# Squared activations without the norm's factor, a smaller setup table in PSUM, one norm step per gated step, and 28 six-product pairs with ten Strassen pairs, in a two-layer S5 and attention encoder

## The chip, the cores and the metric

One core of one Trainium2 chip runs the whole program. The metric is the time of one execution in device microseconds (us), the median of several runs. Shorter names of the engines: PE (TensorE, matrix products), DVE (VectorE), ACT (ScalarE), POOL (GpSimd), SP (SyncE, which here only issues DMA transfers).

## The reference

Two layers on a residual stream of 256 tokens by 2048 channels, all in float32. Layer 0 mixes tokens with a bidirectional diagonal state space (S5), followed by a gated linear unit (GLU); layer 1 with windowed attention. A dense MLP follows each. Every part has an RMS norm ahead of it and a residual addition behind it:

```python
def rms_norm(x, gain):
    y = x * lax.rsqrt(jnp.mean(x * x, axis=-1, keepdims=True) + NORM_EPS)
    return y * gain

def s5_mixer(u, a_re, a_im, log_step, b_re, b_im, c_re, c_im, d_skip, w_glu_a, w_glu_b):
    step = jnp.exp(log_step)[..., None]
    mag = jnp.exp(ar * step)
    lb_re = mag * jnp.cos(ai * step)
    lb_im = mag * jnp.sin(ai * step)
    den = ar * ar + ai * ai
    ...
    z = jax.nn.gelu(y)
    return (z @ w_glu_a) * jax.nn.sigmoid(z @ w_glu_b)

def sqrelu_mlp(h, w_up, w_down):
    return jnp.square(jax.nn.relu(h @ w_up)) @ w_down

for i in range(2):
    h = h + (s5_mixer, windowed_gqa)[i](rms_norm(h, ...), ...)
    h = h + sqrelu_mlp(rms_norm(h, mlp_norm[i]), mlp_w_up[i], mlp_w_down[i])
```
`w_up` is 2048 x 8192 and `w_down` 8192 x 2048, so one MLP reads 128 MB of weights.

## The kernel before

**Products.** A float32 product is made of three matmuls: each factor is split into a high part (a cast) and a low part (the rest), and high x high, low x high and high x low are summed in PSUM (`mm`, L983 to L987). Every weight tile of 128 x 2048 (1 MB) is loaded by SP in a fixed order (`fetch`, L670), cast by ACT (L692) and its low part taken by DVE (L693) or, for 6 and 7 "forms", in `wload_fast` (L696 to L714). The load runs one tile ahead of its use (`wnext`).

**The order** in which each engine runs its instructions is laid out by a planner when the program is built, from the order of the calls and from its own estimates of time. `issue_after` adds an order between two instructions; `interleave` mixes generators of work by rates.

**S5** (0 to some 230 us). `s5_setup` makes tables of powers of the state's factors: `tables()` works out exponential, sine and cosine on DVE and ACT, interleaved with the input norm `norm()`, whose sum over tokens is a matmul (L326) followed by L328; the sine and cosine steps end in L275. `powers()` makes the powers and then three products of them for each half of the partitions (`tab`: L406, L407 and a copy), and copies the first 64 columns into PSUM (`tabp`). `out_tables` prepares further tables on POOL, with a reciprocal on DVE (L435). Then `s5_a(0)` (first half of the groups; products on DVE, L506, eight blocks), a sequential scan on DVE (`s5_scan`), beside it `s5_a(1)` with the products on POOL, the second scan, and the output part.

**GLU** (to 380 us). `glu_rest` runs four blocks of 512 columns. While block cb's products run, the post-processing of block cb-1 is mixed in at rate 0.7 (L874): `glu_post` has four steps, two that gate, add to the residual and start the next norm (`norm_pre`), and two that transpose the result for the MLP and split it into parts (`norm_post`, L758, L761). Block 3 has nine steps, `glu_tail` last.

**MLP** (`mlp`, called twice). The inputs are multiplied by the norm's gain alone; the factor per token, `rstd`, is put in later. `rstd_row` (L772) lays it along the free axis: two diagonal matrices times a matrix of ones on PE (L779). The up phase has 64 blocks of 128 rows of the hidden layer (`up_mm`: L895 and L897, 16 matmuls each). `up_post` turns one block into its activation: ACT copies one part (L902), DVE adds it to the other, DVE takes the maximum with 0 and multiplies by the row of factors (L903), ACT squares (L905).

The down-projection works on 32 *pairs* of such blocks. In a pair the operands form a 2 x 2 matrix of blocks, so four products in eight block multiplications (24 matmuls with the three per block). Strassen's form has seven (21 matmuls): `FORMS`. Six of these (18 matmuls, `SIXTH`) complete a pair of the first half of the columns except for one block of products, which is done later for four pairs at once. Two passes cover the two halves of the columns:

- *Up phase*: `SIX` puts the six products of pairs 0 to 23 behind up blocks 6, 8, 10, 13, 15, 17, 20 and so on, two or three blocks apart.
- *Pass one* (half 0): `PASS[0]` lists 14 items. A negative number is a tile of `wp2`, which holds the left-out products of four six-product pairs (12 matmuls for one tile); the rest are pairs 24 to 31 in plain form (24).
- *Pass two* (half 1): all 32 pairs, nine of them (`FAST`) in Strassen's form.

Strassen's sums stand in four PSUM banks of their own and are added to the residual once in each pass: in pass one by `fold0` (DVE), in pass two by `fold`, which works out four sums on DVE and lets POOL issue accumulating DMAs into the residual (L1027 to L1034). `end` adds the plain sums (L1040), and behind the second MLP stores the output. `norm_end` works out `rstd` for the next part.

Of the kernel before, what the change touches and what calls it, by code (L numbers as in the profile page):

```python
# [10 lines left out]
F32 = mybir.dt.float32  # L11
# [3 lines left out]
ALU = mybir.AluOpType  # L15
AX = mybir.AxisListType

P = 128
# [164 lines left out]
class Kernel:  # L183
# [109 lines left out]
    def s5_setup(self):  # L293
# [14 lines left out]
        self.tab = ar.get("tab", [3, T, G], at=44032)  # L308
# [61 lines left out]
        def tables():  # L370
            are, aim, lst = prm[:, 0], prm[:, 1], prm[:, 2]
            tb4, tb3 = (self.bank().rearrange("p (k g) -> p k g", k=4) for _ in range(2))
            mag, xr, xi, sn, cs = (tp.tile([P, G], F32, name=n) for n in ("mag", "xr", "xi", "sn", "cs"))
# [12 lines left out]
            v.tensor_mul(lam[:, 1, 1], mag, sn)  # L386

        def powers():
            lam, t2 = self.lam, self.t2

            for o, x, n in ((2, 1, 1), (3, 1, 2)):
                ov, av = lam[:, :, o:o + n], lam[:, :, x:x + n]
                br, bi = (lam[:, i:i + 1, x + n - 1:x + n].broadcast_to([P, 2, n, G]) for i in range(2))
                tv = t2[:, :, 0:n]
                v.tensor_mul(ov, av, br)
                v.tensor_mul(tv, av, bi)
                v.tensor_sub(ov[:, 0], ov[:, 0], tv[:, 1])
                v.tensor_add(ov[:, 1], ov[:, 1], tv[:, 0])
            H = P // 2
            tab = self.tab  # L400
            for lo in (0, H):
                s = slice(lo, lo + H)
                lr = lam[s, 0, 1:T + 1][:, ::-1] if lo else lam[s, 0, 1:T + 1]
                li = lam[s, 1, 1:T + 1][:, ::-1] if lo else lam[s, 1, 1:T + 1]
                a.copy(tab[s, 1], lr)
                v.scalar_tensor_tensor(tab[s, 0], lr, -1.0, li, op0=ALU.mult, op1=ALU.subtract)  # L406
                v.tensor_sub(tab[s, 2], li, lr)  # L407
# [11 lines left out]
        u_trans(0)  # L419
        with self.tc.issue_after(self.rs.ins):  # L420
            powers()
        ar.free("xc", "sq", "gn", "dd")

        def out_tables():
# [10 lines left out]
            v.reciprocal(den, den)  # L435
# [24 lines left out]

    def s5_a(self, h):
# [7 lines left out]
        def statein(b, pin):  # L469
            for i in range(0, 8, 4):  # L470
# [11 lines left out]
                if h == 0 and i:  # L482
                    v.tensor_copy(o, bv)
                else:
                    self.evac = a.copy(o, bv)
# [12 lines left out]
        for b in range(8):  # L498
# [3 lines left out]
            for k, src in ((0, bc[:, 1]), (1, bs), (2, bc[:, 0])):  # L502
                tb = self.tabp[k][:, :, g0:g0 + 8] if h == 0 else tab[:, k, :, g0:g0 + 8]
                tb = tb.rearrange("p t (g o) -> p g t o", o=1).broadcast_to([P, 8, T, 16])
                sb = src.rearrange("p g (o c) -> p g o c", o=1).broadcast_to([P, 8, T, 16])
                e.tensor_mul(q[:, :, k], tb, sb)  # L506
                if k == 2:
                    fetch(b + 3)
                yield
# [262 lines left out]
    def rstd_row(self, rb):  # L772

        nc = self.nc
        bk = self.bank()
        for tt in range(2):
            dg = self.small.tile([P, P], F32, name="dg")
            nc.vector.tensor_scalar_mul(dg, self.ident, self.rstd[:, tt:tt + 1])
            nc.tensor.matmul(bk[:, tt * P:(tt + 1) * P], lhsT=self.ones, rhs=dg, start=True, stop=True)  # L779
        nc.vector.tensor_copy(rb, bk[:, :L])  # L780
# [77 lines left out]
    def glu_rest(self):  # L858
        post = None
        for cb in range(4):  # L860
# [17 lines left out]
    def mlp(self, nxt, fin):  # L878
# [4 lines left out]
        rb = pool.tile([P, L], F32, name="rb", bufs=1)  # L883
# [15 lines left out]
        def up_post(fb, bk):  # L899
# [3 lines left out]
            nc.vector.scalar_tensor_tensor(s, s, 0.0, rb, op0=ALU.max, op1=ALU.mult)  # L903
# [65 lines left out]
        def split(kp, a, fast):  # L969
            n = a.shape[1] // 2  # L970
            if kp < 0:
                k = -1 - kp
                h = hTs[0][:, 8 * k + 1:8 * k + 8:2, :P] if k < 4 else hTs[1][:, 8 * k - 31:8 * k - 24:2, :P]
                return halves(a, h, n)
# [34 lines left out]

        def fold0():  # L1010
            p1, q5, q6, q7 = (bks[n] for n in ("p1", "q5", "q6", "q7"))
            v.tensor_add(rs(0, 0), rs(0, 0), p1)
            nc.scalar.copy(ssix, p1)
            v.tensor_sub(ssix, ssix, q6)
            v.tensor_add(rs(0, 1), rs(0, 1), ssix)
            v.tensor_sub(rs(0, 1), rs(0, 1), q5)
            v.tensor_sub(ssix, q7, ssix)
            v.tensor_add(rs(1, 0), rs(1, 0), ssix)
            v.tensor_add(ssix, ssix, q5)
            v.tensor_add(rs(1, 1), rs(1, 1), ssix)  # L1020

        def fold():
            f = ar.get("fo", [4, 512], at=37888)
            c, d, u, w = (f[:, i] for i in range(4))
            g = nc.gpsimd
# [4 lines left out]
            g.dma_start(rs(0, 1), w, accum_op=ALU.add)  # L1030
            v.tensor_sub(u, bks["q7"], u)
            g.dma_start(rs(1, 0), u, accum_op=ALU.add)
            v.tensor_add(d, u, bks["q5"])
            g.dma_start(rs(1, 1), d, accum_op=ALU.add)  # L1034
            ar.free("fo")

        def end(half, t, j):
            cb = half * 2 + j
            cs = slice(cb * 512, (cb + 1) * 512)
            v.tensor_add(self.resid[:, t, cs], self.resid[:, t, cs], bks["x%d" % (2 * t + j + 1)])  # L1040
# [43 lines left out]
        aform = Ring([ar.get("af#%d" % i, [1024], F32R, at=27648 + 1024 * i) for i in range(4)])  # L1084
        more = [extra(at, F32R) for at in (23552, 25600)]
# [565 lines left out]
```

## Time and profile before

| | |
|---|---|
| median of 3 runs | 2024.76 us (2024.04 to 2025.17) |
| the profiled execution, whole | 2024.08 us |
| its span (first to last instruction) | 2022.3 us, mean granted TensorE clock 0.997 |
| S5 part and GLU, until the first MLP's first own matmuls | 0 to 381 us |
| first MLP: up phase, pass one, pass two | 381 to 839, 839 to 900, 900 to 1069 us |
| attention | 1069 to 1333 us |
| second MLP and output | 1337 to 2022 us |
| HBM read | 372.63 MB, 185 GB/s over the span |

How to read the views: the page's first part gives the busy time of each engine. A row of the groups names line, engine, operation, what is written and read and its shape, the count, then busy us, mean ns of one, and the idle time of the engine just before such instructions with what ended it. A row of the chain of waits gives start (us), duration, engine, what and line, with x for how many in a row; a bracket holds a wait and its releaser. A row of the windows begins with the stretch, its length, then busy us and count of PE, of weight loads (PEld), DVE, ACT and POOL, then the granted clock, the share of the DMA engines' time and GB/s. A row of a timeline gives start, duration, engine, line and operation with shapes, and in brackets the wait before it and who ended it. The operations of a matmul overlap, so that the mean of one is longer than its share of the time.

### The profile page before, as it was taken

Reading aid. Unit: us, or ns where it says so; the run is one execution under the profiler, and the core shown is the slowest. Engines: PE = TensorE matmul, PEld = TensorE weight load, DVE = VectorE, ACT = ScalarE, POOL = GpSimd, SP = SyncE. Lnnn points to the kernel's source line nnn. Section 1 sums busy time; section 2 is a strip of 40 time slices with the busy share of each in tenths; the row PEclk is TensorE's granted clock in tenths of the full one; section 3 lists DMA queues with packets and bytes.
Section 4 is the critical chain, followed back from the end, with each engine's and each line's share of the span. In section 5 each row is a group of like instructions: output and inputs, shape, how many; then the busy total and the mean of one; then the engine's idle time right before and its main releaser. Section 6 shows DMA issues by size and latency. Waiting matters only on the chain.

```text
span 2022.3 us, 33471 instructions
## 1 busy us (share of the span) xinstructions
PE 1977.0 (98%) x13646; PEld 1669.5 (83%) x13646; DVE 1635.4 (81%) x2477; ACT 1140.3 (56%) x1404; POOL 235.6 (12%) x207
## 2 busy tenths in 40 slices
PE   5989999999999999999999999999999999999999
PEld 4877788888888888888888777888888888888887
DVE  8889836798888888788887987578888888888885
ACT  5553555465555555665554666445555555555653
POOL 5996740000000000000010000000000000000000
PEclk9999999999999999999999999999999999999999
DMA  3234457555555455665555432475555545576554
GB/s 124 68 98 149 135 188 250 189 230 201 205 196 208 167 208 208 227 253 222 204 183 190 155 104 96 168 268 208 205 202 182 205 165 202 203 259 231 211 194 135
DMA packets 63514, 378.99 MB, mean 187 GB/s; under 512 B 7184, under 2 KB 9520, under 8 KB 22016
## 3 DMA queue, kind: packets, MB, share of 16 engines
q1 hardware_dynamic: 55872, 354.90, 49.0%
q10 hardware_dynamic: 6128, 19.49, 3.0%
q0 software_dynamic: 1360, 2.46, 0.6%
q8 instruction: 107, 1.75, 0.4%
q14 instruction: 47, 0.39, 0.1%
HBM read 372.63 MB, written 2.10 MB: 185 GB/s over the span
## 4 chain that ended last, share of the span: by engine, by line
PE 90%; DVE 5%; POOL 4%; issue 1%; ACT 0%; DMA 0%; ACTq 0%; SPq 0%; POOLq 0%; DVEq 0%
PE bank L986 32%; PE bank L895 23%; PE bank L897 12%; PE bank L731 6%; PE bank L733 6%; PE bank L732 6%; POOL slot L565 1%; POOL slot L506 1%; DVE slot L693 1%; PE bank L1254 1%; PE bank L1296 1%; PE bank L1287 1%; POOL slot L566 1%; DVE bank L547 1%; PE bank L651 0%
## 5 line engine op out<-in xcount | busy, mean ns | idle before, releaser
L693 DVE TENSOR_TENSOR slot<-slot,slot 128x2048 fp32r<-128x2048 f32 (+1 forms) x280 | 601.5, 2153 | 206.0 <-ACT slot L692 198.3
L692 ACT CAST slot<-slot 128x2048 fp32r<-128x2048 f32 (+1 forms) x301 | 519.9, 1734 | 367.5 <-PE bank L986 94.0
L986 PE MATMUL bank<-slot,slot 128*128 128x512 f32 x2532 | 591.1, 390 | 0.0
L986 PEld LDWEIGHTS bank<-slot,slot 128*128 128x128 f32 x2532 | 471.9, 188 | 95.8
L895 PE MATMUL bank<-slot,slot 128*128 128x512 f32 x2048 | 491.4, 390 | 2.1 <-DVE slot L761 2.0
L895 PEld LDWEIGHTS bank<-slot,slot 128*128 128x128 f32 x2048 | 378.9, 188 | 77.8 <-DVE slot L761 2.5
L708 DVE TENSOR_TENSOR slot<-slot,slot 128x2048 fp32r<-128x2048 f32 (+2 forms) x132 | 241.2, 1827 | 49.5 <-ACT slot L707 48.6
L897 PEld LDWEIGHTS bank<-slot,slot 128*128 128x128 f32 x2048 | 263.2, 191 | 10.4
L897 PE MATMUL bank<-slot,slot 128*128 128x256 f32 x2048 | 266.4, 283 | 0.0
L707 ACT CAST slot<-slot 128x2048 fp32r<-128x2048 f32 (+2 forms) x132 | 203.3, 1540 | 67.4 <-DVE slot L712 51.5
L731 PE MATMUL bank<-slot,slot 128*128 128x512 f32 x544 | 216.2, 399 | 1.2 <-ACT slot L825 1.1
L732 PE MATMUL bank<-slot,slot 128*128 128x512 f32 x544 | 213.2, 392 | 0.0
L733 PE MATMUL bank<-slot,slot 128*128 128x512 f32 x544 | 208.6, 393 | 0.7 <-POOL slot L693 0.7
L953 ACT CAST slot<-slot 128x512 fp32r<-128x512 f32 (+2 forms) x188 | 107.7, 593 | 66.0 <-PE bank L986 43.6
L731 PEld LDWEIGHTS bank<-slot,slot 128*128 128x128 f32 x544 | 102.1, 188 | 25.7 <-issue 3.2
L902 ACT COPY slot<-bank 128x256 f32<-128x256 f32 x128 | 47.2, 368 | 134.3 <-PE bank L897 133.9
L954 DVE TENSOR_TENSOR slot<-slot,slot 128x512 fp32r<-128x512 f32 (+2 forms) x188 | 119.0, 655 | 2.6 <-ACT slot L953 2.5
L733 PEld LDWEIGHTS bank<-slot,slot 128*128 128x128 f32 x544 | 101.7, 188 | 23.2 <-POOL slot L693 1.1
L732 PEld LDWEIGHTS bank<-slot,slot 128*128 128x128 f32 x544 | 102.3, 188 | 20.5 <-issue 1.0
L1027 POOL DMA_DIRECT2D slot<-slot x2 | 1.8, 892 | 891.9 <-ACT slot L1026 891.9
L1183 POOL DMA_DIRECT2D slot<-in_pos x1 | 0.8, 784 | 733.0 <-DVE slot L954 733.0
L986 PE MATMUL bank<-slot 128*128 128x512 f32 x342 | 82.6, 389 | 0.0
(243 smaller groups left out, 1866.5 us busy)
## 6 DMA issues: line engine op xcount, KB each, us to landing
slot<-in_wup SPq DMA_DIRECT2D x128, 1024.0 KB, 4.9
slot<-in_wdn SPq DMA_DIRECT2D x128, 1024.0 KB, 5.0
slot<-in_wqkv SPq DMA_DIRECT2D x20, 1024.0 KB, 4.9
slot<-in_wge ACTq DMA_DIRECT2D x32, 512.0 KB, 4.0
slot<-in_wgl SPq DMA_DIRECT2D x16, 1024.0 KB, 6.2
slot<-in_wo SPq DMA_DIRECT2D x16, 1024.0 KB, 4.9
slot<-in_wp SPq DMA_DIRECT2D x12, 1024.0 KB, 5.7
slot<-in_bz SPq DMA_DIRECT2D x16, 336.0 KB, 3.8
```

The lines of the kernel that those rows point to most:

```text
L692: self.cast = self.nc.scalar.copy(hi[:, c], raw[:, c])
L693: (self.nc.gpsimd if e == "g" else self.nc.vector).tensor_sub(lo[:, c], raw[:, c], hi[:, c].bitcast(F32))
L707: self.nc.scalar.copy(hi, x)
L708: v.tensor_sub(lo, x, hi.bitcast(F32))
L731: pe.matmul(out, lhsT=xh, rhs=wh, start=first, stop=False)
L732: pe.matmul(out, lhsT=xl, rhs=wh, start=False, stop=False)
L733: self.dm = pe.matmul(out, lhsT=xh, rhs=wl, start=False, stop=last)
L895: pe.matmul(bk, lhsT=wh[:, kt], rhs=act[:, kt].rearrange("p x c -> p (x c)"), start=(kt == 0), stop=False)
L897: pe.matmul(bk[:, :L], lhsT=wl[:, kt], rhs=act[:, kt, 0], start=False, stop=(kt == KT - 1))
L953: nc.scalar.copy(o[0], h)
L954: v.tensor_sub(o[1], h, o[0].bitcast(F32))
L986: pe.matmul(bank(bk), lhsT=a[x][:, j], rhs=w[y][:, c], start=bk not in begun, stop=stop and y == 1)
```

## The change

- **Squares without the norm's factor.** relu(r x)² is r² relu(x)² for r > 0, so the factor is left out of the activations and the finished sums are multiplied by R = r², per token, where they are added to the residual. `rstd_row` goes; `scales()` (DVE) makes R and -R for the first 128 tokens; `up_post` has a Relu on ACT in place of L903; `fold0` and `end` add with a factor (`into`); `fold` multiplies each sum in place on ACT ahead of its DMA.
- **Pairs.** 28 pairs have six products between the up blocks, behind blocks 6, 8, ..., 60. Pass one has seven `wp2` items and four plain pairs. Pass two has ten Strassen pairs, every third, the last pair 27.
- **Setup.** The cosine stands in PSUM. The table products are written directly into PSUM and for the first 64 columns only (`table(.., 0)`); the other 64 columns go to `tab` at block 4 of `s5_a(0)`, behind its evacuations. The powers are called ahead of the input's transposes, the four copies of factors for the scan (`rotations`) behind them, and the reciprocal L435 behind the first product.
- **GLU.** The rate 0.7 is 1.0: one step of norm work per step of matmuls.

```diff
-SIX = {6 + 7 * p // 3: p for p in range(24)}
-FAST = (0, 4, 7, 10, 13, 16, 20, 23, 26)
-PASS = ((-1, 24, -2, 25, 26, -3, 27, -4, 28, 29, -5, 30, -6, 31), range(32))
+SIX = {6 + 2 * p: p for p in range(28)}
+FAST = (0, 3, 6, 9, 12, 15, 18, 21, 24, 27)
+PASS = ((-1, 28, -2, -3, 29, -4, -5, 30, -6, -7, 31), range(32))
...
-            step = tb4[:, 0]
+            step, cs = tb4[:, 0], tb3[:, 3]
...
-            tab = self.tab
-            for lo in (0, H):
-                s = slice(lo, lo + H)
-                lr = lam[s, 0, 1:T + 1][:, ::-1] if lo else lam[s, 0, 1:T + 1]
-                li = lam[s, 1, 1:T + 1][:, ::-1] if lo else lam[s, 1, 1:T + 1]
-                a.copy(tab[s, 1], lr)
-                v.scalar_tensor_tensor(tab[s, 0], lr, -1.0, li, op0=ALU.mult, op1=ALU.subtract)
-                v.tensor_sub(tab[s, 2], li, lr)
             tabp = [self.bank()[:, :n * T * H].rearrange("p (k t g) -> p k t g", k=n, t=T) for n in (2, 1)]
-            a.copy(tabp[0], tab[:, :2, :, :H])
-            a.copy(tabp[1], tab[:, 2:, :, :H])
             self.tabp = [tabp[0][:, 0], tabp[0][:, 1], tabp[1][:, 0]]
+            self.table(self.tabp, 0)
+
+        def rotations():
+            lam = self.lam
             lb = self.lb = self.bank().rearrange("p (r q g) -> p r q g", r=2, q=2)
...
         scale0()
-        u_trans(0)
         with self.tc.issue_after(self.rs.ins):
             powers()
+        u_trans(0)
+        rotations()
...
-            v.reciprocal(den, den)
+            with self.tc.issue_after(self.first.ins):
+                v.reciprocal(den, den)
...
+    def table(self, out, h):
+        H = P // 2
+        gs = slice(h * H, h * H + H)
+        for lo in (0, H):
+            s = slice(lo, lo + H)
+            lr, li = (self.lam[s, i, 1:T + 1, gs] for i in range(2))
+            if lo:
+                lr, li = lr[:, ::-1], li[:, ::-1]
+            self.nc.vector.scalar_tensor_tensor(out[0][s], lr, -1.0, li, op0=ALU.mult, op1=ALU.subtract)
+            self.nc.scalar.copy(out[1][s], lr)
+            self.nc.vector.tensor_sub(out[2][s], li, lr)
...
                 if k == 2:
                     fetch(b + 3)
+                    if h == 0 and b == 4:
+                        with self.tc.issue_after(self.evac.ins), self.tc.issue_after(self.vevac.ins):
+                            self.table([tab[:, i] for i in range(3)], 1)
...
-    def rstd_row(self, rb):
...
+    def scales(self):
+        v = self.nc.vector
+        self.R = self.small.tile([P, 3], F32, name="rr")
         for tt in range(2):
...
+            ms = self.small.tile([P, 1], F32, name="ms")
+            v.reduce_sum(ms, self.ss[:, tt, :], axis=AX.X)
+            v.tensor_scalar(ms, ms, 1.0 / D, EPS, op0=ALU.mult, op1=ALU.add)
+            v.reciprocal(self.R[:, tt:tt + 1], ms)
+        v.tensor_scalar_mul(self.R[:, 2:3], self.R[:, 0:1], -1.0)
...
-                interleave(mm, (post, 0.7))
+                interleave(mm, (post, 1.0))
...
-            nc.vector.scalar_tensor_tensor(s, s, 0.0, rb, op0=ALU.max, op1=ALU.mult)
+            nc.scalar.activation(s, s, AF.Relu)
...
-        for tt in range(2):
-            self.norm_end(tt)
...
-        self.rstd_row(rb)
...
+        self.scales()
+        R = self.R
...
+        def into(t, j, x, r=None):
+            o = rs(t, j)
+            r = t if r is None else r
+            v.scalar_tensor_tensor(o, x, R[:, r:r + 1], o, op0=ALU.mult, op1=ALU.add)
...
         def fold0():
             p1, q5, q6, q7 = (bks[n] for n in ("p1", "q5", "q6", "q7"))
-            v.tensor_add(rs(0, 0), rs(0, 0), p1)
+            into(0, 0, p1)
...
         def fold():
...
+            def into(t, j, x):
+                nc.scalar.mul(x, x, R[:, t:t + 1])
+                nc.gpsimd.dma_start(rs(t, j), x, accum_op=ALU.add)
             nc.scalar.copy(c, bks["p1"])
-            g.dma_start(rs(0, 0), c, accum_op=ALU.add)
             v.tensor_sub(u, c, bks["q6"])
+            into(0, 0, c)
...
-            v.tensor_add(self.resid[:, t, cs], self.resid[:, t, cs], bks["x%d" % (2 * t + j + 1)])
+            into(t, j, bks["x%d" % (2 * t + j + 1)])
...
+        aform.i = (6 - len(PASS[0])) % 4 - 1
```
The last line sets which of four buffers the ring of split activations begins with.

More of the change, by code (lines that the diff above doesn't have):

```diff
@@ L307, in s5_setup @@
         self.u = [ar.get("u%d" % h, [32, 2, NC], at=(39936, 19456)[h]) for h in range(2)]
-        self.tab = ar.get("tab", [3, T, G], at=44032)
+        self.tab = ar.get("tab", [3, T, G // 2], at=44032)
         self.ta = ar.get("ta", [2, 2 * T, G], at=49664)
@@ L372, in tables @@
             tb4, tb3 = (self.bank().rearrange("p (k g) -> p k g", k=4) for _ in range(2))
-            mag, xr, xi, sn, cs = (tp.tile([P, G], F32, name=n) for n in ("mag", "xr", "xi", "sn", "cs"))
-            step = tb4[:, 0]
+            mag, xr, xi, sn = (tp.tile([P, G], F32, name=n) for n in ("mag", "xr", "xi", "sn"))
+            step, cs = tb4[:, 0], tb3[:, 3]
             lam = self.lam = tb.tile([P, 2, 5, G], F32, name="lam")
@@ L482, in statein @@
                 if h == 0 and i:
-                    v.tensor_copy(o, bv)
+                    self.vevac = v.tensor_copy(o, bv)
                 else:
@@ L502, in s5_a @@
             for k, src in ((0, bc[:, 1]), (1, bs), (2, bc[:, 0])):
-                tb = self.tabp[k][:, :, g0:g0 + 8] if h == 0 else tab[:, k, :, g0:g0 + 8]
+                tb = (tab[:, k] if h else self.tabp[k])[:, :, b * 8:b * 8 + 8]
                 tb = tb.rearrange("p t (g o) -> p g t o", o=1).broadcast_to([P, 8, T, 16])
                 sb = src.rearrange("p g (o c) -> p g o c", o=1).broadcast_to([P, 8, T, 16])
-                e.tensor_mul(q[:, :, k], tb, sb)
+                m = e.tensor_mul(q[:, :, k], tb, sb)
+                if h == 0 and b == 0:
+                    self.first = m
                 if k == 2:
                     fetch(b + 3)
+                    if h == 0 and b == 4:
+                        with self.tc.issue_after(self.evac.ins), self.tc.issue_after(self.vevac.ins):
+                            self.table([tab[:, i] for i in range(3)], 1)
                 yield
@@ L770, in norm_end @@
         self.rsqrt(self.rstd[:, tt:tt + 1], ms, 1)
-    def rstd_row(self, rb):
-        nc = self.nc
-        bk = self.bank()
+    def scales(self):
+        v = self.nc.vector
+        self.R = self.small.tile([P, 3], F32, name="rr")
         for tt in range(2):
[L777 to L780, printed above, removed]
+            ms = self.small.tile([P, 1], F32, name="ms")
[3 more added lines that the diff above has]
+        v.tensor_scalar_mul(self.R[:, 2:3], self.R[:, 0:1], -1.0)
     def zk(self, kt):
@@ L882, in mlp @@
         pool = Scope(ar, "ml", 2, 48128)
-        rb = pool.tile([P, L], F32, name="rb", bufs=1)
         hTs = [ar.get("hT#0", [32, L], at=31744)]
@@ L972, in split @@
                 k = -1 - kp
-                h = hTs[0][:, 8 * k + 1:8 * k + 8:2, :P] if k < 4 else hTs[1][:, 8 * k - 31:8 * k - 24:2, :P]
+                c = 8 * (k if k < 4 else k % 2) + 1
+                h = hTs[max(k // 2 - 1, 0)][:, c:c + 7:2, :P]
                 return halves(a, h, n)
@@ L1008, in rs @@
             return self.resid[:, t, half * 1024 + j * 512:half * 1024 + (j + 1) * 512]
+        def into(t, j, x, r=None):
+            o = rs(t, j)
+            r = t if r is None else r
+            v.scalar_tensor_tensor(o, x, R[:, r:r + 1], o, op0=ALU.mult, op1=ALU.add)
         def fold0():
             p1, q5, q6, q7 = (bks[n] for n in ("p1", "q5", "q6", "q7"))
-            v.tensor_add(rs(0, 0), rs(0, 0), p1)
+            into(0, 0, p1)
             nc.scalar.copy(ssix, p1)
             v.tensor_sub(ssix, ssix, q6)
-            v.tensor_add(rs(0, 1), rs(0, 1), ssix)
-            v.tensor_sub(rs(0, 1), rs(0, 1), q5)
+            into(0, 1, ssix)
+            into(0, 1, q5, 2)
             v.tensor_sub(ssix, q7, ssix)
-            v.tensor_add(rs(1, 0), rs(1, 0), ssix)
+            into(1, 0, ssix)
             v.tensor_add(ssix, ssix, q5)
-            v.tensor_add(rs(1, 1), rs(1, 1), ssix)
+            into(1, 1, ssix)
         def fold():
@@ L1024, in fold @@
             c, d, u, w = (f[:, i] for i in range(4))
-            g = nc.gpsimd
+            def into(t, j, x):
+                nc.scalar.mul(x, x, R[:, t:t + 1])
+                nc.gpsimd.dma_start(rs(t, j), x, accum_op=ALU.add)
             nc.scalar.copy(c, bks["p1"])
-            g.dma_start(rs(0, 0), c, accum_op=ALU.add)
             v.tensor_sub(u, c, bks["q6"])
+            into(0, 0, c)
             v.tensor_sub(w, u, bks["q5"])
-            g.dma_start(rs(0, 1), w, accum_op=ALU.add)
+            into(0, 1, w)
             v.tensor_sub(u, bks["q7"], u)
-            g.dma_start(rs(1, 0), u, accum_op=ALU.add)
             v.tensor_add(d, u, bks["q5"])
-            g.dma_start(rs(1, 1), d, accum_op=ALU.add)
+            into(1, 0, u)
+            into(1, 1, d)
             ar.free("fo")
```

## The prediction

> **What bounds the kernel now.** I read the page first, then the chain of waits, then PE's own waits, then stretches by windows.
>
> ```profile
> span 2022.3 us, 33471 instructions
> ...
> PE 1977.0 (98%) x13646; PEld 1669.5 (83%) x13646; DVE 1635.4 (81%) x2477; ACT 1140.3 (56%) x1404; POOL 235.6 (12%) x207
> ...
> L986 PE MATMUL bank<-slot,slot 128*128 128x512 f32 x2532 | 591.1, 390 | 0.0
> ...
> L986 PE MATMUL bank<-slot 128*128 128x512 f32 x342 | 82.6, 389 | 0.0
> ```
> PE is busy for all but 45 us of the span, and the down-projection's matmuls (L986, 2532 + 342 = 2874) never stood idle before one. The 390 ns in these rows overlap, so the price of one comes from the chain:
>
> ```profile
> 424.19 4.11 PE bank L986 x18
> 428.29 3.63 PE bank L895 x16
> ...
> 475.39 4.11 PE bank L986 x18
> ...
> 839.40 211.51 PE bank L986 x933
> ...
> 1790.50 227.84 PE bank L986 x1005
> ```
> In both long runs one matmul costs 211.51/933 = 227.84/1005 = 0.2267 us, without a break. From one six-product group at 424.19 to the equivalent one at 475.39 is 51.20 us, seven up blocks and three groups. So in both MLPs time is the number of matmuls, as long as their operands are ready. The rest of the idle time is at the start, in the S5 part and at one place ahead of the first MLP:
>
> ```profile
> PE bank L895 <- DVE slot L761: 2.0, 1, 2.0
> ```
>
> **The change part by part.** *Matmuls.* Per MLP, before: 24 groups x 18 = 432 in the up phase; pass one 6 x 12 + 8 x 24 = 264; pass two 9 x 21 + 23 x 24 = 741; sum 1437, twice 2874, which is the page's count. After: 28 x 18 = 504; 7 x 12 + 4 x 24 = 180; 10 x 21 + 22 x 24 = 738; sum 1422. Thirty fewer x 0.2267 = **-6.8 us**, provided that nothing starves PE. A group moved into the up phase costs the same there: 4.11/18 = 0.228 each.
>
> *Does the up phase bear a group at every second block?* Before, the gaps are 2, 2, 3; a stretch of two gaps of 2 shows what the new rhythm asks:
>
> ```profile
> 475.39:505.82 30.43, 30.43 (x166) 26.44 (x165) 26.58 (x31) 17.76 (x21) 0.00 (x0) 1.00 0.48 180
> ...
> L903 DVE SCALAR_TENSOR_TENSOR slot<-slot 128x256 f32<-128x256 f32 x51 | 21.5, 421 | 0.7
> L905 ACT ACTIVATE slot<-slot 128x256 f32<-128x256 f32 x50 | 20.8, 415 | 15.0 <-DVE slot L903 14.6
> ```
> DVE (third busy figure) has 26.58 of 30.43 us, 87%. The change takes L903 away from every up block (four here, 1.7 us) and gives ACT a Relu of about L905's 0.42 (17.8 + 1.7 = 19.4 of 30.43). DVE falls to 82%, so I cost the denser rhythm at nothing; its cover is DVE's 5 us of slack in 30. Weights per time hardly change (ten tiles in 51.2 us against three in 15.2).
>
> *Pass one* is where cover is thin: seven of its eleven items give PE only 12 x 0.2267 = 2.72 us for a whole 1 MB tile.
>
> ```profile
> 839.24:880.34 41.10, 41.10 (x184) 34.02 (x183) 31.07 (x26) 26.05 (x25) 0.00 (x0) 1.00 0.76 286
> ...
> 854.50 2.29 DVE L693 TENSOR_TENSOR slot<-slot,slot 128x2048 fp32r<-128x2048 f32 x1 [2.75 <-ACT slot L692]
> 858.36 2.29 DVE L693 TENSOR_TENSOR slot<-slot,slot 128x2048 fp32r<-128x2048 f32 x1 [1.57 <-ACT slot L692]
> 861.17 4.49 DVE L693 TENSOR_TENSOR slot<-slot,slot 128x2048 fp32r<-128x2048 f32 x2
> ```
> Pass one begins at 839.24. Counting one L693 per tile, its items 5, 6 and 7 have their low parts at 856.8, 860.7 and 863.4, that is 17.6, 21.4 and 24.2 us in. Here DMA, cast and raw buffers set the pace, not PE. The new order wants them at 19.0, 21.8 and 24.5, plus 0.45 since the low part feeds the third matmul. So the rate already seen just suffices, with 0.7 us to spare at items 6 and 7; item 8 is due only at 29.9. DVE must also do `fold0` (eight operations) between block 60 and pass one, one block later than now. I allow **+0.5 us** for both MLPs together; bounds 0 and 3 us in each.
>
> [...]
>
> *Pass two*: three matmuls fewer; Strassen pairs now at every third pair throughout, as most are already. The last is pair 27, so `fold` runs one plain pair (5.4 us) later and each of its four sums is scaled on ACT (about 0.6) ahead of its DMA.
>
> ```profile
> 1996.80 1.02 POOL L1034 DMA_DIRECT2D slot<-slot  x1
> ...
> 2018.37 0.69 DVE L1040 TENSOR_TENSOR slot<-slot,bank 128x512 f32<-128x512 f32 x1 [2.03 <-PE bank L986]
> ```
> The last accumulation is issued at 1996.8; moved by 6 to 7 us it is issued at about 2003.5, 15 us ahead of the addition at 2018.37 that reads its block; DVE's queue behind it holds only the ends. Nothing. That last addition gets a per-row factor; I take its 0.69 as 0.74: **+0.05**.
>
> *Entry of the MLPs.* The row of the norm goes: two multiplications of the identity on DVE and two matmuls with `ones`, which stand on PE's path in both MLPs:
>
> ```profile
> 393.10 0.45 PE bank L779 x4
> ...
> 1346.98 0.45 PE bank L779 x4
> ```
> 2 x 0.45 = **-0.9 us**. The new `scales` (seven tiny DVE operations) is first used at `fold0`, hundreds of us later: nothing.
>
> *One norm step per gated step.* In column block 3 the rate 0.7 puts both transposes of block 2 behind the whole tail, and their splits (L761) are what the first up block waits for:
>
> ```profile
> 368.50 0.69 DVE L749 TENSOR_TENSOR slot<-slot,slot 128x512 f32<-128x512 f32 x1
> ...
> 380.47 1.03 PE L758 MATMUL bank<-ident,slot 128*128 128x128 f32 x8
> 381.26 2.09 PE L895 MATMUL bank<-slot,slot 128*128 128x512 f32 x8
> 385.40 1.21 PE L895 MATMUL bank<-slot,slot 128*128 128x512 f32 x4 [2.05 <-DVE slot L761]
> 387.88 0.60 PE L758 MATMUL bank<-ident,slot 128*128 128x128 f32 x4
> ```
> Their input was ready at 369.2 (L749). At rate 1.0 they come 5 to 10 us earlier, between tail matmuls, and the 2.05 us go. Next late is block 3's own transpose (387.88), whose DVE chain gets 1.2 us of L761 out of its way but which PE then reaches 2 us sooner. I take **-1.7**, bounds 0 and -2.05.
>
> *Setup.*
>
> ```profile
> 10.54 4.55 POOL L335 TENSOR_TENSOR slot<-slot,slot 128x2048 f32<-128x2048 f32 x1 [9.23 <-DMA slot<-in_xc]
> 13.19 1.98 DVE L275 TENSOR_SCALAR slot<-slot 128x128 f32<-128x128 f32 x1
> 15.71 0.59 PE L326 MATMUL bank<-slot,slot 128*128 128x4 f32 x2 [4.31 <-ACT slot L321]
> 17.40 0.15 DVE L328 TENSOR_SCALAR slot<-bank 128x4 f32<-128x4 f32 x1
> 25.58 0.51 POOL L433 TENSOR_TENSOR slot<-slot 128x128 f32<-128x128 f32 x1 [6.93 <-DVE slot L397]
> 25.86 0.77 DVE L406 SCALAR_TENSOR_TENSOR slot<-slot 64x512 f32<-64x512 f32 x1
> 28.23 0.94 DVE L407 TENSOR_TENSOR slot<-slot 64x512 f32<-64x512 f32 x1
> 29.20 0.95 DVE L435 RECIPROCAL slot<-slot 128x128 f32<-128x128 f32 x1
> 30.07 3.62 DVE L506 TENSOR_TENSOR slot<-bank,slot 128x512 f32<-128x512 f32 x6
> ```
> L275 lasts until POOL's long product ends (15.09); its result now goes to PSUM, where nothing of POOL's lies; L903, with twice its elements, takes 0.42, so I take 0.3. That frees 1.7 us; the norm's sum (L326, done at 16.3) is then next, so everything behind L328 moves by some 1.4 us. The four table operations (25.86 to 29.17) shrink to half their columns, about 0.42 each like L903, saving 1.7; the reciprocal steps behind the first product, saving 0.95. The first product thus comes 4.1 us earlier. The other half of the table is four such operations later, at block 4 of the state inputs (1.7 us of DVE). How much arrives at the end depends on two chains:
>
> ```profile
> 120.08 2.12 POOL slot L506 x2
> ...
> 136.14 2.04 PE bank L638 x64
> ...
> 136.45 1.38 DVE L625 COPY slot<-slot 64x504 f32<-64x504 f32 x2
> ```
> The chain that decides runs through POOL (its products until 122.2, then PE until 138.2); DVE's scan is done 1.7 us sooner, at 136.45, which also covers the moved table. POOL starts only 1.4 us earlier (L433 waits for the powers), so the bounds are 1.4 and 4.1; nearer to the lower, as that chain binds, I take **-2.5**; 0 stays in the range, as the planner lays out every queue anew.
>
> *Sum:* -6.8 + 0.5 + 0.05 - 0.9 - 1.7 - 2.5 = **-11.35 us**. The profiled execution took 2024.08 us (span 2022.3), 0.7 below the median 2024.76; the same difference on the median gives **2013.4**.
>
> **Rivals.** *A: pass one starves.* If the later `fold0` and the denser groups delay the tiles by more than the 0.7 us to spare, PE waits once per MLP, some 3 us: +6, about 2019. For it: the margins above; against: DVE's 82% before.
>
> *B: the setup's gain is lost* between POOL's chain and the S5 part behind it: 2.5 less, 2015.9. For it: the deciding chain is POOL's; against: POOL itself starts earlier.
>
> *C: the setup gives more*, since PE's clock no longer drops:
>
> ```profile
> 30.40:33.10 2.70, 0.98 (x6) 0.56 (x5) 2.70 (x6) 1.98 (x6) 2.39 (x6) 0.98 0.00 0
> 33.10:36.94 3.84, 3.80 (x19) 3.63 (x20) 2.43 (x4) 1.50 (x3) 3.64 (x4) 0.57 0.66 214
> ```
> PE is idle most of 30.4 to 33.1, and then the granted clock is 0.57 for 19 transposes in 3.8 us, where 8 of them at L758 take 1.03, 2.4 for 19. If the idle stretch closes and POOL's waits shrink too, 4.7 instead of 2.5: 2011.2. [...]
>
> *D: slower.* The place is the up phase: 28 groups in each MLP, where ACT now has three steps behind each up block (copy, Relu, square) and DVE waits for its casts. If that chain needs more than a group's 15.2 us, each of 56 groups pays: 0.2 us eats the whole gain, 0.28 makes the kernel slower by 0.2%, and 0.5 would give 2013.4 + 28 = 2041. It needs 2.6 us of new waiting in every 15.2; against it stands PE's unbroken run in stretches with just these gaps.
>
> **How the numbers follow.** Forecast 50%, A 17%, B 16%, C 12%, D 5%. A change of 0.2%, about what a measurement of this kernel can tell from none, is 4.05 us, so the forecast, B, C and most of A (2019) are faster: 0.92; the tail of A and the mild part of D: 0.05 the same; D else: 0.03. The range takes in A, B and C with their bounds: 2009.5 to 2019.5.
>
> **What would show it.** 2844 matmuls at the down-projection's line, still 0.227 apart, none waiting in pass one or between blocks 6 and 60. No PE wait at the first MLP's entry. The cosine's last step at about 0.3 us, the first S5 product near 26, the last inner product of the first half (now ending at 138.2) some 2.5 us sooner. Wrong would be PE idle ahead of the first `wp2` items, a `fold` that holds the ends, or groups over 15.2 us apart.

## The result and the profile after

The changed kernel took **2012.01 us** (median of four runs, 2010.74 to 2013.36), against 2024.63 (2024.04 to 2025.17): 12.6 us less, ratio 0.9938 with a 95% interval of 0.9924 to 0.9951. The forecast was 11.35 us less. The profiled execution was the longest of the four, 2013.36 us. Lines of `kernel.py` have moved: L986 is now L1000, L895 L909, L506 L515, L693 L707, L761 L775.

The page of the changed kernel, then the two rows of the groups view for the down-projection (busy us, mean ns, idle time before):

```profile
span 2011.6 us, 33347 instructions
...
PE 1967.4 (98%) x13608; PEld 1664.1 (83%) x13608; DVE 1638.5 (81%) x2403; ACT 1209.0 (60%) x1564; POOL 235.1 (12%) x207
```
```profile
L1000 PE MATMUL bank<-slot,slot 128*128 128x512 f32 x2532 | 592.6, 390 | 0.0
...
L1000 PE MATMUL bank<-slot 128*128 128x512 f32 x312 | 77.4, 390 | 0.0
```
2532 + 312 = 2844 matmuls, none after an idle stretch. The chain of waits (start, duration) shows both long runs, 918 matmuls at 208.11/918 = 0.2267 us:

```profile
421.08 4.11 PE bank L1000 x18
...
852.62 208.11 PE bank L1000 x918
1368.02 4.11 PE bank L1000 x18
...
1799.56 208.12 PE bank L1000 x918
```
These rows divide the span. "First up block" is the start of the first matmul of the first MLP, less the transposes that stand ahead of it (0.79 us before; after, two sets of four stand among the GLU's matmuls, at 0.36 each).

| profiled execution | before | after | change |
|---|---|---|---|
| span's start to first up block | 380.47 | 380.33 | -0.14 |
| to the first six-product group | 43.72 | 40.75 | -2.97 |
| to the second MLP's first group | 951.09 | 946.94 | -4.15 |
| to the end of the last down-projection | 643.06 | 639.66 | -3.40 |
| to the end of the span | 3.96 | 3.92 | -0.04 |

So the last two thirds did about as forecast, the entry of the first MLP gave more, and the first 380 us, where the setup was to bring 2.5, gave nothing in this execution. PE's waits behind 145 us are down to two, both in the S5 part; neither MLP has one:

```profile
PE bank L745 <- ACT slot L840: 2.4, 1, 2.4
PE bank L665 <- DVE slot L639: 0.6, 1, 0.6
```
Windows of two groups of the up phase and of pass one (PE, PEld, DVE, ACT, POOL busy; clock, DMA share, GB/s):

```profile
466.72:497.14 30.42, 30.42 (x165) 26.45 (x165) 25.65 (x28) 19.10 (x26) 0.00 (x0) 1.00 0.56 208
```
```profile
862.00:870.00 8.00, 8.00 (x37) 6.64 (x36) 3.96 (x5) 4.29 (x3) 0.00 (x0) 1.00 0.98 396
```
DVE fell from 26.58 to 25.65 of 30.4 us, ACT rose to 19.10 (forecast 19.4). In pass one the DMA engines are at 0.98 and 396 GB/s.

In the setup (timeline of DVE) the cosine's last step takes 0.29 instead of 1.98, and the first product (L515) starts at 27.23 instead of 30.07. The table's second half is at 47.72:

```profile
13.38 0.29 DVE L275 TENSOR_SCALAR bank<-slot 128x128 f32<-128x128 f32 x1
...
27.23 0.69 DVE L515 TENSOR_TENSOR slot<-bank,slot 128x512 f32<-128x512 f32 x1
...
47.72 0.85 DVE L466 SCALAR_TENSOR_TENSOR slot<-slot 64x256 f32<-64x256 f32 x1
48.49 0.41 DVE L468 TENSOR_TENSOR slot<-slot 64x256 f32<-64x256 f32 x1
48.91 0.66 DVE L466 SCALAR_TENSOR_TENSOR slot<-slot 64x256 f32<-64x256 f32 x1
49.49 1.34 DVE L468 TENSOR_TENSOR slot<-slot 64x256 f32<-64x256 f32 x1
```
Behind that first product the lead is lost again in this execution. Two things stand there. ACT's output-table steps (L452) wait for POOL and stand in front of an evacuation (L494) that PE needs:

```profile
36.33 2.55 ACT L452 ACTIVATE slot<-slot 64x512 f32<-64x512 f32 x4 [2.66 <-POOL slot L285]
38.90 0.59 ACT L494 COPY slot<-bank 128x512 f32<-128x512 f32 x1
```
and PE, idle for it, comes back at a lower granted clock (0.76, then 0.82):

```profile
38.00:42.00 4.00, 2.46 (x54) 2.46 (x56) 1.53 (x3) 3.82 (x8) 3.26 (x4) 0.76 0.48 165
42.00:46.00 4.00, 4.00 (x66) 3.71 (x65) 2.59 (x5) 2.72 (x5) 4.00 (x5) 0.82 0.02 6
```
The state inputs end at 67.34 instead of 65.90.

### The profile page after: what moved, and what is told of

Its sections match the earlier page's. It is cut to its first block, busy times and chain, and to the rows that moved or that the text cites. A ratio compares the mean times of both kernels' runs of the same rounds, so it can differ in the third digit from the quotient of the medians.

```text
span 2011.6 us, 33347 instructions
## 1 busy us (share of the span) xinstructions
PE 1967.4 (98%) x13608; PEld 1664.1 (83%) x13608; DVE 1638.5 (81%) x2403; ACT 1209.0 (60%) x1564; POOL 235.1 (12%) x207
## 3 DMA queue, kind: packets, MB, share of 16 engines
q0 software_dynamic: 1360, 2.46, 0.7%
## 4 chain that ended last, share of the span: by engine, by line
PE 92%; DVE 3%; POOL 2%; ACT 1%; DMA 1%; issue 1%; ACTq 0%; SPq 0%; POOLq 0%; DVEq 0%
PE bank L1000 32%; PE bank L909 23%; PE bank L911 12%; PE bank L745 6%; PE bank L747 6%; PE bank L746 6%; PE bank L1277 1%; PE bank L1319 1%; PE bank L487 1%; DVE slot L707 1%; PE bank L1310 1%; POOL slot L515 1%; PE bank L601 1%; POOL slot L579 1%; PE bank L539 1%
## 5 line engine op out<-in xcount | busy, mean ns | idle before, releaser
L707 DVE TENSOR_TENSOR slot<-slot,slot 128x2048 fp32r<-128x2048 f32 (+1 forms) x272 | 584.6, 2153 | 187.0 <-ACT slot L706 179.8
L706 ACT CAST slot<-slot 128x2048 fp32r<-128x2048 f32 (+1 forms) x293 | 504.7, 1729 | 324.1 <-PE bank L909 112.8
L1000 PE MATMUL bank<-slot,slot 128*128 128x512 f32 x2532 | 592.6, 390 | 0.0
L1000 PEld LDWEIGHTS bank<-slot,slot 128*128 128x128 f32 x2532 | 472.0, 188 | 95.1
L909 PE MATMUL bank<-slot,slot 128*128 128x512 f32 x2048 | 489.8, 391 | 0.0
L909 PEld LDWEIGHTS bank<-slot,slot 128*128 128x128 f32 x2048 | 379.8, 188 | 75.3
L722 DVE TENSOR_TENSOR slot<-slot,slot 128x2048 fp32r<-128x2048 f32 (+2 forms) x152 | 277.2, 1824 | 48.7 <-ACT slot L721 48.6
L721 ACT CAST slot<-slot 128x2048 fp32r<-128x2048 f32 (+2 forms) x152 | 233.7, 1537 | 51.8 <-DVE slot L726 39.0
L967 DVE TENSOR_TENSOR slot<-slot,slot 128x512 fp32r<-128x512 f32 (+2 forms) x198 | 124.3, 651 | 6.6 <-ACT slot L966 6.2
L1047 POOL DMA_DIRECT2D slot<-slot x8 | 7.0, 970 | 915.9 <-ACT slot L1046 915.9
L726 DVE TENSOR_TENSOR slot<-slot 128x1024 f32<-128x1024 f32 x76 | 92.7, 1219 | 0.3
```

The costliest lines, as they stand in the source:

```text
L706: self.cast = self.nc.scalar.copy(hi[:, c], raw[:, c])
L707: (self.nc.gpsimd if e == "g" else self.nc.vector).tensor_sub(lo[:, c], raw[:, c], hi[:, c].bitcast(F32))
L721: self.nc.scalar.copy(hi, x)
L722: v.tensor_sub(lo, x, hi.bitcast(F32))
L909: pe.matmul(bk, lhsT=wh[:, kt], rhs=act[:, kt].rearrange("p x c -> p (x c)"), start=(kt == 0), stop=False)
L967: v.tensor_sub(o[1], h, o[0].bitcast(F32))
```

## The experiments

Each was timed beside the kernel before; "ratio" is to that, with its 95% interval, and a difference given behind it is worked out from the ratio. Line numbers differ from run to run by one or two.

**The lists of pairs alone** (mm_only), on the kernel before.
```diff
-SIX = {6 + 7 * p // 3: p for p in range(24)}
+SIX = {6 + 2 * p: p for p in range(28)}
...
```


> The kernel before with the new lists of pairs alone (28 six-product pairs, 11 items in pass one, ten Strassen pairs); DVE still multiplies each up block by the norm's factor. Theory 1 (time is the number of matmuls): 30 x 0.2267 = 6.8 us less, 2017.8. Theory 2 (the denser rhythm needs the lighter up block): the up phase has waits on PE ahead of the groups, and less than 5 us are gained. Theory 3 (pass one starves without the other changes): a wait of 1 to 3 us on PE in each pass one, 2020 or more.

2017.28 us, ratio 0.9966 (0.9954 to 0.9979): -6.9. From the first group to the second MLP's first group 947.70, -3.39; from there to the last matmul 639.66, -3.40. PE has no new wait in either MLP (the old one of 2.05 us at the first entry stays), though DVE still had L903. Theory 1.

**The factor-free squares alone** (norm_only), on the kernel before.
```diff
-            nc.vector.scalar_tensor_tensor(s, s, 0.0, rb, op0=ALU.max, op1=ALU.mult)
+            nc.scalar.activation(s, s, AF.Relu)
...
-        self.rstd_row(rb)
```


> The kernel before with the factor-free squares alone (no row of factors, Relu on ACT, the sums multiplied by R where they are added to the residual). Theory 1 (only the two products with the ones at each MLP's entry stood on the path): 0.9 us less. Theory 2 (the lighter up block on DVE shortens the up phase): more than 2 us less. Theory 3 (the scaled fold or the three steps on ACT cost time): 0 or longer, with waits on PE in the up phase or ahead of the last matmuls.

2022.63 us, ratio 0.9993 (0.9984 to 1.0002). The timing can't tell it from nothing; the trace can: 43.26 instead of 43.72 at the first MLP's entry (-0.46), 950.38 instead of 951.09 up to the second one (-0.71), the rest equal. Theory 1, at 1.17 instead of 0.9.

**The rate alone** (rate_only), on the kernel before.
```diff
-                interleave(mm, (post, 0.7))
+                interleave(mm, (post, 1.0))
```


> The kernel before with the rate of the gated part's norm steps at 1.0 alone. Theory 1 (the wait of 2.05 us ahead of the first up blocks goes, nothing takes its place): 2.05 to 2.5 us less, the latter as the matmuls just behind that idle stretch no longer start slowly. Theory 2 (as predicted, part of it comes back as a wait for block 3's own transposes): 1.7 less, with a wait on the last splits visible near 386 us. Theory 3: nothing, as the transposes then delay the tail's matmuls by as much.

2021.14 us, ratio 0.9984 (0.9975 to 0.9993): -3.2. From the first up block to the first group 41.18 instead of 43.72, -2.54, and no wait on the splits. Theory 1.

**The setup**, taken out of the changed kernel (no_setup), and put alone on the kernel before (setup_only).
```diff
+            step, cs = tb4[:, 0], tb3[:, 3]
...
+            self.table(self.tabp, 0)
```


> The changed kernel with the whole S5 setup of before. Theory 1 (the new setup gains 2.8 us at the first product and gives it back by the end of the S5 part): within 0.7 us of the changed kernel. Theory 2 (as predicted, the setup is worth 2.5 us): 2.5 us longer, about 2014.5. Theory 3 (the moved half of the table costs more than the setup saves): 1 to 2 us shorter.

> The kernel before with the new S5 setup alone. Theory 1 (gain given back): 2024.6 less 0 to 0.7 us. Theory 2 (as predicted): 2022.1. Theory 3 (net loss): over 2025.5. In the profile the first product of the state inputs starts near 27.2 us in all three; they part at the end of the state inputs (66.6 before).

Without it 2013.3 us, ratio 0.9944 (0.9932 to 0.9957), 1.7 longer than the changed kernel timed beside it (after_again below, 2011.56) and 1.3 longer than its first timing; alone 2024.9, ratio 1.0001 (0.9992 to 1.0009). In the trace of the latter, S5 and GLU did end earlier, but the old wait at the MLP's entry then met a drop of the clock (timeline of PE and a window):

```profile
383.81 1.58 PE L909 MATMUL bank<-slot,slot 128*128 128x512 f32 x4 [2.05 <-DVE slot L775]
385.18 2.76 PE L911 MATMUL bank<-slot,slot 128*128 128x256 f32 x12
```
```profile
384.00:388.00 4.00, 4.00 (x19) 3.73 (x18) 3.94 (x18) 1.45 (x4) 0.00 (x0) 0.57 1.01 422
```
The twelve matmuls of 1.59 us took 2.76; the entry took 45.22 us instead of 43.72. In the profile before, the same idle 2.05 us were followed by a clock of 1.00. The first comparison lies between theories 1 and 2. The second has the time of theory 1; in the traced execution this drop cost 1.5 us of it, and whether the other ten executions had one is not known.

**The changed kernel again** (after_again), no edit.

> The changed kernel itself, a second time, beside the others. Its first profile (2013.36 us) was the longest of four runs that lie between 2010.74 and 2013.36. Theory 1 (the setup's gain is lost by the order of instructions): the second profile has the same waits in the first 140 us, the inner products of the first half end near 140 us again, and the time is 2011 to 2013. Theory 2 (it was lost in that one execution, to transfers that came late): they end near 136 and the time is near 2010.5.

2011.56 us (five runs, 2010.66 to 2013.62), ratio 0.9936 (0.9923 to 0.9950). The inner products end at 137.29, between the two theories: much the same waits, but other places of the low clock, and the first up block 2.16 us earlier. So about as much as was sought changes from one execution to the next. The next table has all profiled executions with either setup unaltered, in us: the start of the first product on DVE (L506 or L515), the end of PE's state inputs of the first half (L478 or L487), the end of its inner products of the first half (L638 or L652), and the first up block as above.

| | first product | state inputs end | inner products end | first up block |
|---|---|---|---|---|
| old: before | 30.07 | 65.90 | 138.16 | 380.47 |
| old: no_setup | 30.33 | 65.36 | 137.43 | 380.27 |
| old: mm_only | 30.29 | 65.67 | 140.75 | 383.25 |
| old: rate_only | 30.13 | 65.86 | 139.61 | 382.11 |
| old: norm_only | 30.35 | 65.69 | 137.51 | 379.66 |
| new: after | 27.23 | 67.34 | 140.05 | 380.33 |
| new: after_again | 26.98 | 65.53 | 137.29 | 378.17 |
| new: setup_only | 26.89 | 65.00 | 137.17 | 378.88 |
| new: wp2_row | 27.00 | 65.35 | 138.19 | 380.04 |
| new: up_twice | 26.83 | 64.96 | 137.55 | 380.30 |
| new: fast11 | 27.06 | 65.20 | 138.64 | 378.91 |
| mean, new less old | -3.2 | -0.1 | -0.5 | -1.7 |

With a spread of 1.5 (old) and 0.9 us (new), the last difference of means has a standard error of some 0.8. Part of the scatter goes with the clock: its record in the traces shows 2, 2, 3, 3 and 4 stretches of 3.41 us at half clock ahead of the first up block with the old setup, and 1, 2, 2, 2, 3 and 4 with the new one. A straight-line fit over the eleven executions puts about 0.8 us (± 0.3) on each stretch and leaves 1.3 (± 0.6) for the setup. The lead of 3.2 us is gone where the state inputs end; a part of it shows again behind them.

**ACT's table steps behind the evacuation** (ta_late), on the changed kernel.
```diff
-                    a.mul(ta[x * H:(x + 1) * H, k, dr * T:(dr + 1) * T], src, sg)
+                    with self.tc.issue_after(ev.ins):
+                        a.mul(ta[x * H:(x + 1) * H, k, dr * T:(dr + 1) * T], src, sg)
```
(`ev` is the last evacuation issued when these steps begin.)

> The changed kernel with one move on ACT: its eight output-table steps (which wait for POOL near 36 us) are ordered behind the first evacuation of the state inputs. Theory 1 (these steps in front of that evacuation give back the setup's gain: PE waits 2 us there, its clock then drops): that wait is gone, the second set of state inputs starts near 36.5 instead of 39.5 us, the state inputs end 2 to 3 us sooner, and the time is 1 to 2.5 us below the changed kernel. Theory 2 (the gain is cut off by what follows in any case, POOL's products and the waits at the gated part's first blocks): the state inputs end sooner, but the first up block does not start sooner, and the time is within 0.7 us of the changed kernel.

2012.84 us, ratio 0.9941 (0.9928 to 0.9953): no gain. The second set of state inputs began at 36.95, as theory 1 has it, but the next four steps held the next evacuation (1.58 us of PE's time), the moved table then took from 45.35 to 49.54, and the state inputs ended at 66.05. The time is theory 2's, but the state inputs ended no sooner either.

**DVE spared the table's second half** (half_free), on the changed kernel. ACT copies the first half's values into its place, so the second half of the groups gets other powers than its own.
```diff
-                            self.table([tab[:, i] for i in range(3)], 1)
+                            for i in range(3):
+                                a.copy(tab[:, i], self.tabp[i])
```


> The changed kernel without DVE's four operations for the second half of the table: ACT copies the first half's values into their place, so the second half of the groups is computed from the wrong powers. It prices that moved piece. Theory 1 (the piece holds DVE for 3 to 4 us, not 1.7, as its operations wait for POOL's, and PE behind it for over 1 us): the state inputs end 2 to 3 us sooner than in the changed kernel (66.4 to 68.2 there), and, as the scan follows, the time is 1.5 to 2.5 us lower. Theory 2 (the moved piece is covered by PE's steady 3.9 us per block): less than 1 us at the end of the state inputs. Theory 3 (what is gained here is lost again at the first gated blocks, whose banks wait for ACT behind DVE): the state inputs end 2 to 3 us sooner, but the first up block starts within 0.7 us of the changed kernel's 378.9 to 381.1.

2012.16 us, ratio 0.9937 (0.9923 to 0.9950). DVE's scan (L562 here) starts at 64.47 instead of 66.38 or 68.18, and PE's state inputs end at 63.63; yet the inner products end at 137.90 and the first up block is at 380.92. The times are those of theory 3: nothing of it arrives. The cause is another than that theory names. The shifts of the states behind the scan, half of them on DVE and half on ACT, began on DVE 1.9 us sooner than in after_again (134.18, 136.09), but PE waited 1.95 us for the first one on ACT, 0.6 more than there. The rows show what stood in front of it on ACT:

```profile
134.18 1.38 DVE L640 COPY slot<-slot 64x504 f32<-64x504 f32 x2
...
135.97 0.59 ACT L620 COPY slot<-bank 128x512 f32<-128x512 f32 x1 [3.53 <-PE bank L602]
137.00 2.06 ACTq L701 DMA_DIRECT2D slot<-in_wge  x3
139.18 2.52 ACT L640 COPY slot<-slot 64x504 f32<-64x504 f32 x4 [2.62 <-DVE slot L563]
```
The shift on ACT stands behind a copy that waits for PE (L602) and behind three DMA issues for the GLU's weights. (The releaser in its bracket is inferred; that operation of DVE had ended at 137.6.) In thirteen of the fourteen traces of this case ACT's first shift begins 0.11 to 0.13 us behind these issues, and 0.2 to 5.4 us behind DVE's. So the scan is not what PE waits for there. No run moves the issues, so what they cost is not measured.

**POOL's tables earlier** (pool_early), on the changed kernel.
```diff
-            t0, t1 = t2[:, 0, 0], t2[:, 1, 0]
+            t0, t1 = (tp.tile([P, G], F32, name=n) for n in ("ex_k", "sc_r"))
...
-            with self.tc.issue_after(self.first.ins):
-                v.reciprocal(den, den)
+            v.reciprocal(den, den)
```


> The changed kernel with two things in POOL's output tables: their two scratch tiles are no longer those of the powers (so that POOL needn't wait 6.9 us for DVE's last use of them, to 24.66 us), and the reciprocal is not held back behind the first product. [...] Theory 1 (POOL's chain is what sets the end of the first half, so that what the setup brings is what POOL starts earlier): POOL's tables are done some 5 us sooner than 40.5, the state inputs end 1 us later, the inner products end 1 to 3 us before the changed kernel's 137.2 to 140.1, and the time is 0.5 to 2 us lower. Theory 2 (the scan on DVE and the gated part's first blocks set the end): POOL is earlier, but the inner products end no sooner than 137 and the first up block starts within 1 us of 379.4 (the mean of the changed kernel's setups), or later.

2021.69 us, ratio 0.9980 (0.9971 to 0.9990): some 9 us worse than the changed kernel. Neither theory has this: POOL's tables were done at 39.9, hardly sooner than the 40.5 of the changed kernel. POOL's table products now lie beside DVE's, and the first half of the table, 24.94 to 27.20 us in the changed kernel, took from 27.52 to 32.32 (timeline of DVE):

```profile
28.01 2.91 DVE L467 TENSOR_TENSOR bank<-slot 64x256 f32<-64x256 f32 x2
30.82 1.50 DVE L465 SCALAR_TENSOR_TENSOR bank<-slot 64x256 f32<-64x256 f32 x1
```
ACT's evacuations stood behind a copy of that table; PE, busy for 0.71 of the 4 us from 30 on, ran at half clock (0.50), by the clock's record from 32.15 to 42.39:

```profile
34.00:38.00 4.00, 1.50 (x6) 0.72 (x5) 2.03 (x4) 3.92 (x10) 1.12 (x2) 0.50 0.60 169
38.00:42.00 4.00, 3.85 (x18) 3.85 (x19) 1.90 (x3) 3.95 (x9) 2.21 (x3) 0.50 0.19 69
```
The scan began at 76.25, 8 to 10 us late, and the first up block, at 388.79, was 9 us late. This is the one trace in which ACT's first shift waits for the scan. Together with half_free: a scan 8 to 10 us later costs in full, one 2 us sooner brings nothing, as the rows of half_free have ACT's shift behind other work.

**All left-out products at the head of pass one** (wp2_row), on the changed kernel.
```diff
-PASS = ((-1, 28, -2, -3, 29, -4, -5, 30, -6, -7, 31), range(32))
+PASS = ((-1, -2, -3, -4, -5, -6, -7, 28, 29, 30, 31), range(32))
```


> The changed kernel with all seven items of left-out products at the head of pass one, so that PE uses seven tiles of 1 MB in 7 x 2.72 = 19.0 us instead of over 40 us; no work is added. Theory 1 (pass one has next to no spare time: DVE needs 2.29 for a tile's low part and 0.68 for the item's split, 2.97 per item, and DMA at the 394 GB/s seen there 2.66): PE waits in both pass ones, 7 x 0.25 = 1.7 us less what was prepared ahead, 0 to 2 us in each. [...] Theory 3 (the waiting is longer, since four raw buffers and the fixed order of loads hold the next tiles back): 3 to 6 us in each.

2016.65 us, ratio 0.9959 (0.9944 to 0.9974). One wait in each pass one (timeline of PE, then the window around it):

```profile
862.25 2.56 PE L1000 MATMUL bank<-slot,slot 128*128 128x512 f32 x10 [1.29 <-DVE slot L707]
...
1810.77 2.60 PE L1000 MATMUL bank<-slot,slot 128*128 128x512 f32 x10 [1.28 <-DVE slot L707]
```
```profile
860.00:870.00 10.00, 8.71 (x39) 6.90 (x38) 8.26 (x7) 6.03 (x5) 0.00 (x0) 1.00 1.01 397
```
Each costs the stretch 1.6 us (948.52 for 946.94, 641.28 for 639.66). Theory 1: with the DMA engines full (share 1.01), the tiles for seven such items in a row do not all come in time.

**The maximum twice** (up_twice), on the changed kernel.
```diff
             nc.scalar.activation(s, s, AF.Relu)
+            nc.vector.tensor_scalar_max(s, s, 0.0)
```


> The changed kernel with the maximum taken a second time, on DVE, between ACT's Relu and the square: the chain behind an up block is longer by one operation of 0.42 us and one change of engine, and DVE has 26.58 + 0.7 or so of 30.43 us again. Theory 1 (DVE's and ACT's slack in the up phase covers it): within 0.2% of the changed kernel, no waits on PE in the up phase. Theory 2 (the chain from block to six-product group is what the denser rhythm hangs on): waits on PE ahead of the groups, 0.2 to 0.5 us for each of 56, 11 to 28 us in all.

2012.58 us, ratio 0.9940 (0.9927 to 0.9954). No wait in the up phase, 946.98 and 639.66 us for the two stretches. Theory 1.

**Eleven Strassen pairs** (fast11), on the changed kernel.
```diff
-FAST = (0, 3, 6, 9, 12, 15, 18, 21, 24, 27)
+FAST = (0, 3, 5, 8, 11, 14, 16, 19, 22, 24, 27)
```


> The changed kernel with eleven Strassen pairs in pass two (0, 3, 5, 8, 11, 14, 16, 19, 22, 24, 27), three matmuls fewer in each MLP. Theory 1 (time is still the number of matmuls): 6 x 0.2267 = 1.4 us less. Theory 2 (DVE, busy for 28.8 of 30 us in the first part of pass two, becomes the bound, as one more such pair costs it some 5.7 us there): PE waits on low parts in pass two, the gain is lost, and the time is the same or up to 6 us longer.

2015.5 us, ratio 0.9956 (0.9943 to 0.9970), 3 to 4 us longer. Theory 2: PE waits for DVE where two such pairs stand two apart (timeline of PE):

```profile
977.28 7.09 PE L1000 MATMUL bank<-slot,slot 128*128 128x512 f32 x30 [0.53 <-DVE slot L707]
...
1022.35 1.65 PE L1000 MATMUL bank<-slot 128*128 128x512 f32 x6 [1.26 <-DVE slot L967]
```

No version tried beat the changed kernel.

## Why the prediction was right, point by point

- *Matmuls* (-6.8): measured -6.80, 3.40 in each MLP, to 0.02 us in every execution. The rhythm of a group at every second block is covered, with more to spare than was counted (up_twice).
- *Pass one* (+0.5 allowed, bounds 0 to 3): nothing. The order of the change mixes `wp2` items with plain pairs, and that is what keeps it from waiting; wp2_row shows 1.6 us at once without it. From 862 to 870 us the DMA engines moved 396 GB/s at a share of 0.98, and PE was busy throughout.
- *The end* (+0.05): -0.04; the last accumulating DMA was issued at about 1994.9, sooner even than before (1996.8), where 2003.5 was forecast; the order was laid out anew. The last addition took 0.75 us, against 0.69 before.
- *Row of factors* (-0.9): -1.17. Right in kind; in the second MLP its absence closed a further 0.26 us that the 0.45 of the products does not contain.
- *GLU entry* (-1.7, bounds 0 and -2.05): -2.54. The step that failed is "next late is block 3's own transpose": no such wait came. The transposes of block 2 now stand in the tail, and block 3's chain was ready in time:

```profile
369.88 0.60 PE L772 MATMUL bank<-ident,slot 128*128 128x128 f32 x4
...
375.12 0.60 PE L772 MATMUL bank<-ident,slot 128*128 128x128 f32 x4
...
381.05 2.88 PE L909 MATMUL bank<-slot,slot 128*128 128x512 f32 x12
...
385.20 0.60 PE L772 MATMUL bank<-ident,slot 128*128 128x128 f32 x4
```
  The bound was too tight as well: a stall shown as 2.05 us costs 2.46, as the eighth matmul's modelled end hides 0.28 of it and the first four behind it took 1.04 instead of 0.91. (12 matmuls from 381.05 to 383.77 are 2.72; before, from 381.26 to 386.44, 5.18.)
- *Setup* (-2.5, bounds 1.4 and 4.1, 0 in the range): about -1.7 ± 0.8 over eleven executions, -0.14 in the first profile; the timings give 0 (setup_only) and -1.3 to -1.7 (no_setup). The 2.5 lies just within that uncertainty, but its terms were mis-sized. The first product came 2.84 us sooner in the first profile, not 4.1: step L328 came 0.86 sooner instead of 1.4, and the first half of the table took 2.29 (24.94 to 27.23) instead of 1.7. The moved half, "four such operations, 1.7 us of DVE", took 3.1 us in both profiles of the changed kernel and 4.2 in ta_late, and PE waited 1.1 us for it. The prediction saw that L275 ends with POOL's L335 (1.98 us beside its 4.55; with the result in PSUM 0.29, beside 4.57), and did not see that the table's operations would lie beside POOL's products. In the traces the moved half's L466 and L468, which read both inputs from slots in SBUF, take from 0.41 us (at 48.49, where POOL is idle from 48.28 to 48.83) to 1.34, and 1.49 in ta_late; the products L515, one of whose inputs is in PSUM, take 0.63 to 0.69 throughout in the first profile. No run isolates what makes the difference.
- *Setup, what arrives.* That the end lacks just what the moved half took is not shown: half_free, without it, is no faster. That the chain through POOL binds and the scan does not is borne out; its start moved by 0.9 us (POOL's first table product, 24.66 for 25.58) instead of 1.4, and the end of POOL's tables by 1.9 (40.52 for 42.42). What the prediction did not have in that chain is its last link, the copy and the DMA issues ahead of ACT's shift.
- *Rivals.* A (pass one starves) and D (up phase bound by its chain) are excluded by traces without one wait. B came true in the first profile and in part on the mean. C's price was near the total, but its mechanism was not there: the clock still dropped, at other places (at 40.05 us in the first profile, at 33.00 before, where PE had been busy for 0.52 of the 3.41 us ahead of it).

The sum by measured terms: -6.8 - 1.17 - 2.54 - 1.7 = -12.2, for 12.6 and 12.9 in the two timings.

## What to carry to other kernels

Where PE runs without a break, count matmuls: the price of one from the chain times the number was right to hundredths of a microsecond here, and the room for it is tested by doubling the cheapest suspect. A time saved on one of the chains that lead out of a region is worth only what the last of them gives up: follow each to its end, an engine's own queue included, and ask of each moved operation what will run beside it at its new place. Where the first part of a kernel scatters by more than the gain sought, compare several profiles at fixed marks, not one.

## What was not expected of the hardware

Nearly all scatter of this program is in its first 380 us: the same code reached the first up block at 379.66 to 383.25 (old setup), while the 950 and 640 us behind it repeat to 0.1 us (but for 0.5 us in pool_early), and the entry between them differed once, in setup_only. The granted clock falls at other places in the two profiled executions of the changed kernel, here behind 102 us (the same window; its matmuls are not the same, as the work lies some 2 us apart):

```profile
102.00:108.00 6.00, 4.60 (x74) 4.25 (x76) 5.45 (x17) 1.66 (x3) 6.00 (x6) 0.74 0.19 38
```
```profile
102.00:108.00 6.00, 6.00 (x229) 5.42 (x229) 5.45 (x17) 3.33 (x6) 6.00 (x7) 1.00 0.35 112
```
And one idle stretch of 2.05 us is followed by a granted clock of 0.57 in one execution (setup_only) and of 1.00 in another (before). The clock's record shows steps: in before and after each change lies a whole number of 3.41 us behind the first one, and the stretches at half clock (0.50) are 3.41 us long; in pool_early one is three times that, 32.15 to 42.39. Laid on these steps, the stall left PE busy for 0.40 of one step in setup_only, where the clock dropped, and for 0.64 or more of each in before, where it did not. No step ahead of a drop was wholly idle: in before and after PE was busy for 0.37 to 0.75 of it. So that share alone does not decide, and what does is not shown.
